# HGRN2 weights inside a chunk: from units of four levels to doubling levels on two column groups of the array

## The chip, the cores and the metric

The kernel runs on one core of a Trainium2 chip. The metric is the device time in microseconds. TensorE is PE, VectorE is DVE, ScalarE is ACT, GpSimd is POOL; PSUM is the memory that PE writes, SBUF the one all engines read.

## The reference

Two layers over 256 tokens of width 2048. Each projects the normalised input, mixes it in two branches of eight heads (a gated delta rule, DN, and HGRN2, HG), projects back, and adds a gated embedding. All is float32. The part that changes is the HGRN2 recurrence within a chunk:

```python
G = jnp.cumsum(log_f, axis=3)
...
rel = masked_exp(causal, G_c[:, :, :, None, :] - G_c[:, :, None, :, :])
A = jnp.einsum("bhrd,bhsd,bhrsd->bhrs", q_c, k_c, rel)
o = (jnp.einsum("bhrd,bhde->bhre", qd_c, state)
     + jnp.einsum("bhrs,bhse->bhre", A, v_c))
```

For every pair r >= s of tokens, A[r, s] is the sum over 128 channels of q[r] k[s] exp(G[r] - G[s]). The exponential depends on r, s and the channel, so A is no plain matrix product. It is one for any block of pairs that have a common token m with s <= m < r: q[r] exp(G[r] - G[m]) times k[s] exp(G[m] - G[s]), and neither exponent is positive.

## The kernel before

Weights of the projections (stages `in`, `out`, `gate`, `up`) are streamed by SP's DMA queue as `raw` tiles. ACT rounds each to F32R (`whi`, L366), DVE forms the rest (`wlo`, L368), and PE sums three products per tile: whi by the activations' high part, wlo by the high part, whi by the low part. Twelve such matmuls, of 512 columns mostly, make a step of `run_step`; `ahead` loads four steps and prepares (whi, wlo) two steps before PE needs them.

The stage `in` runs in 17 chunks of columns. When a chunk is complete, generators (`DN`, `HG`, one per group of two heads and layer, four of each per layer) are started on it. They run between the steps: each `yield` gives a number of steps to wait (`tick`), from the tables `DELAY` and `DELAY_AT`, where "h0a" is step `a` of HG group 0. PE executes in the order written (`keep_in_program_order`); the queues of DVE, ACT and POOL are put in order by a scheduler.

`HG.f_side` makes k and G (a scan along tokens) for a group: two heads by two chunks of 128 tokens, four 128x128 blocks, channels on partitions. `HG.q_side` makes the weights A (tokens s on partitions, r along the free axis), four 128x128 blocks:

- The diagonal: four matmuls of k by q (`pad`), of which the mask `ident` keeps s = r.
- Units u = 1, 4, 16 (`quads`, `quad_products`): in each block of 4u tokens, the pairs of different units of u. K is k decayed to its unit's end (POOL's difference, an Exp, a product with k); Q is q decayed back to the end of each of the three earlier units (three differences, an Exp of 768, three products on DVE). Four matmuls of 192 moving columns, in two PSUM tiles; then DVE places what belongs with `copy_predicated` under masks `ms`, six a unit.
- Level 64 (`halves(64)`): four matmuls with 64 stationary and 64 moving columns; and between the two chunks (`halves(128)`) two of 128 columns (`pax`). POOL makes one of the differences of each.
- `po` multiplies A by the values; `head_norm` follows.

In the profile a matmul's names stand as out <- moving, stationary. Plain F32 matmuls are two records each on PE.

Of the kernel before, what the change touches and what calls it, by code (L numbers as in the profile page):

```python
# [25 lines left out]
def chunk_cols(chunk):  # L26
# [8 lines left out]
    "h": {'c': 1, 'f': 1, 'a': 3, 'u': 1, 'u1': 2, 'u4': 2, 'u16': 2, 'x': 2, 'o': 1, 'y': 2, 'yp': 1, 'q': 0, 'K': 0},  # L35
# [96 lines left out]
UNITS = (1, 4, 16)  # L132


NMASK = 128 + 3 * 192


def const_arrays():
    i = np.arange(128)
    c = np.zeros((128, 4 * 128 + 256), np.float32)  # L140
# [4 lines left out]
    c[:, 512:768] = (np.arange(256) % 128 != 0)[None, :]  # L145
    s, r = i[:, None], i[None, :]
    m = np.zeros((128, NMASK), np.int32)
    m[:, 0:128] = (s // 32 == r // 32) & (s % 32 < 16) & (r % 32 >= 16)
    for n, u in enumerate(UNITS):
        o = 128 + 192 * n  # L150
        for d in (1, 2, 3):
            full = (s // (4 * u) == r // (4 * u)) & (s // u % 4 + d == r // u % 4)
            w = (4 - d) * 128 // 4
            m[:, o:o + w] = full.reshape(128, -1, 4 * u)[:, :, d * u:].reshape(128, w)
            o += w
    return c, m
# [3 lines left out]
def trunk(ctx: ExitStack, tc: tile.TileContext, head, xT, x, pT, W, par, fw, cst, msk, eye, out):  # L160
# [4 lines left out]
    ap_ = pool("acts", 15)  # L165
# [14 lines left out]
    cs = cp.tile([128, 768], F32, name="cs")  # L180
# [68 lines left out]
    keep = cs[:, 512:768]  # L249
# [26 lines left out]
    def bc1(ap, n):  # L276
        return ap.unsqueeze(1).to_broadcast([ap.shape[0], n, ap.shape[1]])
# [549 lines left out]
    class HG:  # L827
# [42 lines left out]
        def q_side(self, qr):  # L870
            l, g, n = self.l, self.g, self.n
            q = mix("hq", 512, 1, n + "q")
            sigmoid(q, qr)
            V.tensor_tensor(q, qr, q, ALU.mult)
            yield self.after("f")
            k, Gc = self.k, self.G
            G4, k4, q4 = v4(Gc), v4(k), v4(q)

            def quads(u):


                nb = 512 // (4 * u)
                vu = lambda ap: ap.rearrange("p (n a b) -> p n a b", a=4, b=u)
                ends = vu(Gc)[:, :, :, u - 1:u]
                K = k
                if u > 1:
                    K = mix("hX", 512, 2, n + f"K{u}")
                    v2 = lambda ap: ap.rearrange("p (n b) -> p n b", b=u)
                    G.tensor_tensor(v2(K), v2(Gc)[:, :, u - 1:u].to_broadcast([128, 512 // u, u]), v2(Gc), ALU.subtract)
                    S.activation(K, K, AF.Exp)  # L890
                    V.tensor_tensor(K, K, k, ALU.mult)
                Q = mix("hQ", 768, 1, n + f"Q{u}")
                Q6 = Q.rearrange("p (n x) -> p n x", x=6 * u)
                o = 0
                for d in (1, 2, 3):
                    w = 4 - d
                    V.tensor_tensor(Q6[:, :, o:o + w * u].rearrange("p n (a b) -> p n a b", b=u), vu(Gc)[:, :, d:],
                                    ends[:, :, :w].to_broadcast([128, nb, w, u]), ALU.subtract)
                    o += w * u
                S.activation(Q, Q, AF.Exp)  # L900
                o = 0
                for d in (1, 2, 3):
                    w = 4 - d
                    V.tensor_tensor(Q6[:, :, o:o + w * u], Q6[:, :, o:o + w * u],
                                    q.rearrange("p (n x) -> p n x", x=4 * u)[:, :, d * u:], ALU.mult)
                    o += w * u
                return K, Q

            def quad_products(u, K, Q):
                for hh in range(2):  # L910
                    pa = pm.tile([128, 512], F32, tag="m", name=n + f"pa{u}_{hh}")
                    for t in range(2):
                        PE.matmul(pa[:, 192 * t:192 * t + 192], v4(K)[:, 2 * hh + t],
                                  Q[:, 384 * hh + 192 * t:384 * hh + 192 * t + 192], start=True, stop=True)
                    P6 = pa[:, :384].rearrange("p (i n x) -> p i n x", i=2, x=6 * u)
                    Av = A[:, 2 * hh:2 * hh + 2].rearrange("p i (n x) -> p i n x", x=4 * u)
                    o, mo = 0, 128 + 192 * UNITS.index(u)
                    for d in (1, 2, 3):
                        w = (4 - d) * u
                        mk = ms[:, mo:mo + 32 * (4 - d)].rearrange("p (n x) -> p n x", x=w)  # L920
                        V.copy_predicated(Av[:, :, :, d * u:], mk.unsqueeze(1).to_broadcast([128, 2, 32 // u, w]),
                                          P6[:, :, :, o:o + w])
                        o += w
                        mo += 32 * (4 - d)

            def halves(hb):

                X = mix("hX", 512, 2, n + f"X{hb}")
                X4 = v4(X)
                if hb == 64:  # L930
                    mid = G4[:, :, 63:64].to_broadcast([128, 4, 64])
                    lo, hi = (slice(None), slice(None), slice(0, 64)), (slice(None), slice(None), slice(64, 128))
                    G.tensor_tensor(X4[lo], mid, G4[lo], ALU.subtract)
                    V.tensor_tensor(X4[hi], G4[hi], mid, ALU.subtract)
                else:
                    lo, hi = (slice(None), slice(0, None, 2)), (slice(None), slice(1, None, 2))
                    G.tensor_tensor(X4[lo], G4[:, 0::2, 127:128].to_broadcast([128, 2, 128]), G4[lo], ALU.subtract)
                    V.tensor_copy(X4[hi], G4[hi])
                S.activation(X, X, AF.Exp)
                V.tensor_tensor(X4[lo], X4[lo], k4[lo], ALU.mult)  # L940
                V.tensor_tensor(X4[hi], X4[hi], q4[hi], ALU.mult)
                return X

            if self.wait("q"):
                yield self.wait("q")
            KQ = quads(1)
            yield self.wait("a")
            A = v4(mix("hA", 512, 1, n + "A"))
            pa = pm.tile([128, 512], F32, tag="m", name=n + "pad")
            for i in range(4):  # L950
                PE.matmul(pa[:, 128 * i:128 * i + 128], k4[:, i], q4[:, i], start=True, stop=True)
            V.tensor_tensor(A, v4(pa), bc1(ident, 4), ALU.mult)
            yield self.wait("u")
            for u in UNITS:
                if self.wait("K"):
                    yield self.wait("K")
                nxt = quads(4 * u) if u < 16 else halves(64)
                quad_products(u, *KQ)
                KQ = nxt
                yield self.wait(f"u{u}")  # L960
            X4 = v4(KQ)
            X = halves(128)
            pa = pm.tile([128, 512], F32, tag="m", name=n + "pa64")
            for i in range(4):
                PE.matmul(pa[0:64, 64 * i:64 * i + 64], X4[:, i, 0:64], X4[:, i, 64:128], start=True, stop=True)
            V.tensor_copy(A[0:64, :, 64:128], pa[0:64, :256].rearrange("p (a b) -> p a b", b=64))
            yield self.wait("x")

            X4 = v4(X)
            pa = pm.tile([128, 512], F32, tag="m", name=n + "pax")  # L970
            for hh in range(2):
                PE.matmul(pa[:, 128 * hh:128 * hh + 128], X4[:, 2 * hh], X4[:, 2 * hh + 1], start=True, stop=True)
            Ax = v4(mix("hAx", 256, 1, n + "Ax"))
            S.copy(Ax, v4(pa)[:, 0:2])
# [293 lines left out]
```

## Time and profile before

| what | before |
|---|---|
| runs | 1299.11 us median of 3 (1297.9 to 1301.97) |
| profiled execution | 1301.33 us, span 1299.6 us |
| PE busy | 98% of the span, 6600 records |
| DVE, ACT, POOL busy | 74%, 60%, 8% |
| granted clock of TensorE, mean | 0.996 |
| longest wait of PE behind the start | 2.9 us, for a wlo of DVE |

In the rows quoted below, a timeline row reads: start in us, duration in us, engine, line, operation, out <- in, partitions x elements, and xN where N records in a row are merged (the duration is then from the first start to the last end); in brackets the idle time of the engine before it and what ended it. A matmul's record is longer than the distance to the next, since matmuls are pipelined. A row of a windows view reads: the stretch, its length, then for each engine its busy time and, in parentheses, its records; then the granted clock of PE and DMA figures. A row of groups reads: busy us, mean ns of one | idle time before them and what ended it.

### The profile page before, as it was taken

How to read it: one execution, taken by the hardware profiler on the slowest of the kernel's cores; microseconds unless marked ns; L12 is line 12 of the kernel's file. 1: busy time of each engine (PE TensorE's matmuls, PEld its weight loads, DVE VectorE, ACT ScalarE, POOL GpSimd, SP SyncE). 2: the span in 40 equal slices, each digit the busy share in tenths (PEclk: the TensorE clock that was granted, in tenths of full speed). 3: DMA queues.
4: the chain of work that ended last, by engine and by line, in shares of the span. 5: the costliest groups of instructions: out<-in, count | busy, mean ns of one | idle time of the engine just before them, and what ended most of it. 6: DMA issues, size and time to landing. Idle time of an engine off the chain costs nothing.

```text
span 1299.6 us, 18426 instructions
## 1 busy us (share of the span) xinstructions
PE 1274.4 (98%) x6600; PEld 1067.9 (82%) x6600; DVE 961.0 (74%) x1800; ACT 779.4 (60%) x1392; POOL 103.0 (8%) x86
## 2 busy tenths in 40 slices
PE   8999999999999999999999999999999999999996
PEld 7987788888888888888888887888888888888885
DVE  7788877976798766546668897788877968565475
ACT  7665765666665654447557666657566666444464
POOL 0101010010001110000001100111100002000010
PEclk9999999999999999999999999999999999999998
DMA  8565455445455455565555454544455444655563
GB/s 281 180 208 169 153 158 162 133 151 182 154 163 162 132 163 178 187 192 184 188 184 174 155 162 159 170 142 141 156 184 176 145 163 133 198 179 181 192 194 130
DMA packets 78748, 221.02 MB, mean 170 GB/s; under 512 B 15552, under 2 KB 25152, under 8 KB 78656
## 3 DMA queue, kind: packets, MB, share of 16 engines
q1 hardware_dynamic: 59840, 212.36, 50.4%
q10 hardware_dynamic: 18816, 7.48, 2.2%
q8 instruction: 52, 0.85, 0.3%
q14 instruction: 40, 0.33, 0.1%
HBM read 215.09 MB, written 4.72 MB: 169 GB/s over the span
## 4 chain that ended last, share of the span: by engine, by line
PE 78%; DVE 14%; ACT 3%; issue 2%; DMA 2%; SPq 0%; ACTq 0%; DVEq 0%
PE gate L309 13%; PE out L309 12%; PE in1dv L309 6%; PE in1hf L309 5%; PE in0dk L309 5%; PE in0dv L309 5%; PE in0hf L309 5%; PE in1dk L309 5%; DVE wlo L368 4%; PE in1hi L309 4%; PE in0hi L309 3%; PE up L309 2%; PE in0dz L309 1%; PE in1dz L309 1%; ACT whi L366 1%
## 5 line engine op out<-in xcount | busy, mean ns | idle before, releaser
L368 DVE TENSOR_TENSOR wlo<-raw,whi 128x1024 fp32r<-128x1024 f32 (+1 forms) x394 | 481.8, 1226 | 237.2 <-ACT whi L366 236.2
L366 ACT ACTIVATE whi<-raw 128x1024 fp32r<-128x1024 f32 (+1 forms) x394 | 413.3, 1051 | 342.7 <-PE out L309 83.2
L309 PE MATMUL in1hf<-whi,n1hi 128*128 128x512 f32 x128 | 52.0, 407 | 0.0
L309 PE MATMUL in1hi<-whi,n1hi 128*128 128x512 f32 x128 | 52.0, 406 | 0.0
L309 PE MATMUL in1dk<-whi,n1hi 128*128 128x512 f32 x128 | 51.1, 399 | 0.0
L309 PE MATMUL in1dk<-wlo,n1hi 128*128 128x512 f32 x128 | 50.1, 392 | 0.9 <-DVE wlo L368 0.8
L309 PE MATMUL in1hi<-wlo,n1hi 128*128 128x512 f32 x128 | 50.1, 391 | 0.6 <-DVE wlo L368 0.6
L309 PE MATMUL gate<-whi,g0hi 128*128 128x512 f32 x128 | 50.1, 392 | 0.0
L309 PE MATMUL in1hf<-whi,n1lo 128*128 128x512 f32 x128 | 50.1, 391 | 0.0
L309 PE MATMUL in1hi<-whi,n1lo 128*128 128x512 f32 x128 | 50.0, 391 | 0.0
L309 PE MATMUL in1hf<-wlo,n1hi 128*128 128x512 f32 x128 | 49.9, 390 | 0.0
L309 PE MATMUL in1dk<-whi,n1lo 128*128 128x512 f32 x128 | 49.9, 390 | 0.0
L309 PE MATMUL gate<-whi,g1hi 128*128 128x512 f32 x128 | 49.9, 390 | 0.0
L309 PE MATMUL gate<-whi,g0lo 128*128 128x512 f32 x128 | 49.8, 389 | 0.0
L309 PE MATMUL gate<-wlo,g0hi 128*128 128x512 f32 x128 | 49.8, 389 | 0.0
L309 PE MATMUL gate<-whi,g1lo 128*128 128x512 f32 x128 | 49.8, 389 | 0.0
L309 PE MATMUL gate<-wlo,g1hi 128*128 128x512 f32 x128 | 49.8, 389 | 0.0
L309 PE MATMUL in1dv<-whi,n1hi 128*128 128x512 f32 (+1 forms) x128 | 48.7, 380 | 0.0
L309 PE MATMUL in1dv<-wlo,n1hi 128*128 128x512 f32 (+1 forms) x128 | 46.6, 364 | 0.1
L309 PE MATMUL in1dv<-whi,n1lo 128*128 128x512 f32 (+1 forms) x128 | 46.5, 364 | 0.0
L309 PE MATMUL in0dk<-wlo,n0hi 128*128 128x512 f32 x96 | 38.2, 398 | 2.9 <-DVE wlo L368 2.9
L309 PE MATMUL in0hf<-whi,n0hi 128*128 128x512 f32 x96 | 39.0, 406 | 0.0
(1620 smaller groups left out, 3353.8 us busy)
## 6 DMA issues: line engine op xcount, KB each, us to landing
raw<-W SPq DMA_DIRECT2D x384, 512.0 KB, 3.5
raw<-W SPq DMA_DIRECT2D x7, 544.0 KB, 3.7
h<-x SPq DMA_DIRECT2D x4, 512.0 KB, 5.6
xt<-xT SPq DMA_DIRECT2D x3, 512.0 KB, 7.3
out_dram<-h SPq DMA_DIRECT2D x6, 256.0 KB, 2.2
fw<-fw ACTq DMA_DIRECT2D x2, 512.0 KB, 4.9
pin<-pT ACTq DMA_DIRECT2D x2, 256.0 KB, 3.0
out_dram<-h ACTq DMA_DIRECT2D x2, 256.0 KB, 2.9
```

The source lines that it names most:

```text
L309: return tc.keep_in_program_order(nc.tensor.matmul(*a, **k))
L366: S.activation(hi[:, sl], raw[:, sl], AF.Copy)
L368: V.tensor_tensor(lo[:, sl], raw[:, sl], hi[:, sl].bitcast(F32), ALU.subtract)
```

## The change

The weights of a chunk are made in doubling levels u = 1, 2, 4, 8, 16, 32, 64 (and 128 between the chunks). At level u, each block of 2u tokens has a lower half, whose k is decayed to that half's end, and an upper half, whose q is decayed back to it; `factors` writes both into one tile X in place of K and Q. For u below 64 a 128-token block is two matmuls, one for each 64 tokens, with 64 stationary columns (all of X's tokens there) and as moving columns the 32 of the upper halves. Their outputs lie on PSUM partitions 0 to 63 and 64 to 127, so they use the array's columns 0 to 63 and 64 to 127. The diagonal is in the first of them: q and the level-1 factors stand side by side in a tile of 96 columns per 64 tokens. The masks become six of 32 columns, and results gather in `Ad` (two 64x64 blocks one above the other), which ACT copies to `hA`, a tile that is allocated once and zeroed below its diagonal. Levels are done in the pairs (1, 2), (4, 8), (16, 32), (64, 128), four bursts on PE. All differences are on DVE.

`DELAY` and `DELAY_AT` are set anew, for DN's steps too, and the pool of activations has 13 buffers for 15. The diff, cut:

```diff
-    "h": {'c': 1, 'f': 1, 'a': 3, 'u': 1, 'u1': 2, 'u4': 2, 'u16': 2, 'x': 2, 'o': 1, 'y': 2, 'yp': 1, 'q': 0, 'K': 0},
+    "h": {'c': 1, 'f': 1, 'a': 4, 'u1': 3, 'u4': 3, 'u16': 3, 'o': 2, 'y': 2, 'yp': 1, 'q': 0},
...
-UNITS = (1, 4, 16)
-NMASK = 128 + 3 * 192
+UNITS = (1, 2, 4, 8, 16, 32)
+NMASK = 128 + 32 * len(UNITS)
...
-    ap_ = pool("acts", 15)
+    ap_ = pool("acts", 13)
...
+    hA = cp.tile([128, 4, 128], F32, name="hA")
     def clear_scratch():
+        G.memset(hA[64:128, :, 0:64], 0.0)
...
+            q8 = mix("hq", 768, 1, n + "q").rearrange("p (a c) -> p a c", c=96)
+            q = q8[:, :, 0:64]
...
+            def factors(us):
+                X = mix("hX", 1024, 2, n + f"X{us[0]}")[:, :512 * len(us)]
+                xs = [X[:, 512 * j:512 * j + 512] for j in range(len(us))]
+                for u, x in zip(us, xs):
+                    ends = lo(Gc, u)[:, :, u - 1:u].to_broadcast([128, 256 // u, u])
+                    V.tensor_tensor(lo(x, u), ends, lo(Gc, u), ALU.subtract)
+                    if u < 128:
+                        V.tensor_tensor(hi(x, u), hi(Gc, u), ends, ALU.subtract)
+                    else:
+                        V.tensor_copy(hi(x, u), hi(Gc, u))
+                S.activation(X, X, AF.Exp)
+                for u, x in zip(us, xs):
+                    V.tensor_tensor(lo(x, u), lo(x, u), lo(k, u), ALU.mult)
...
+                    V.tensor_tensor(hx, hx, hx_q, ALU.mult)
+                return [v4(x) for x in xs]
+            def products(us, xs, pa, o=0):
+                for j, (u, x) in enumerate(zip(us, xs)):
+                    for i in range(4):
+                        for b in (0, 64):
+                            xb = x[:, i, b:b + 64]
+                            c = o + 128 * j + 32 * i
+                            PE.matmul(pa[b:b + 64, c:c + 32], xb,
+                                      xb.rearrange("p (n a b) -> p n a b", a=2, b=u)[:, :, 1], start=True, stop=True)
+            def place(us, ws):
...
+                    V.copy_predicated(Ad.rearrange("p i (n a b) -> p i n a b", a=2, b=u)[:, :, :, 1],
+                                      mk.unsqueeze(1).to_broadcast([128, 4, 32 // u, u]),
+                                      w.rearrange("p i (n b) -> p i n b", b=u))
...
+            x1 = q8[:, :, 64:96]
+            V.tensor_tensor(x1, c32(hi(Gc, 1)), c32(lo(Gc, 1)), ALU.subtract)
+            S.activation(x1, x1, AF.Exp)
+            V.tensor_tensor(x1, x1, hq(1)[:, :, :, 0], ALU.mult)
+            xs = factors((2,))
             yield self.wait("a")
+            Ad = mix("hAd", 256, 1, n + "Ad").rearrange("p (i c) -> p i c", i=4)
+            pa = bank("1")
             for i in range(4):
+                for b in (0, 64):
+                    PE.matmul(pa[b:b + 64, 96 * i:96 * i + 96], k4[:, i, b:b + 64], q8[:, 2 * i + b // 64, :],
+                              start=True, stop=True)
+            nxt = factors((4, 8))
+            products((2,), xs, pa, 384)
+            w1 = pa[:, :384].rearrange("p (i c) -> p i c", c=96)
+            V.tensor_tensor(Ad, w1[:, :, 0:64], bc1(ident64, 4), ALU.mult)
+            place((1, 2), (w1[:, :, 64:96], v32(pa[:, 384:512])))
+            yield self.wait("u1")
+            for us, then in (((4, 8), (16, 32)), ((16, 32), (64, 128))):
+                xs, nxt = nxt, factors(then)
+                pa = bank(f"{us[0]}")
+                products(us, xs, pa)
+                place(us, (v32(pa[:, 0:128]), v32(pa[:, 128:256])))
+                yield self.wait(f"u{us[0]}")
...
+            A = hA
+            for b in (0, 64):
+                S.copy(A[b:b + 64, :, b:b + 64], Ad[b:b + 64])
+            S.copy(A[0:64, :, 64:128], pa[0:64, :256].rearrange("p (a b) -> p a b", b=64))
```

How instructions move, for the first group of the first layer (`hg00`). On PE before, the diagonal's four matmuls stand ahead of a step; a burst of the units stands further on (first lines the diagonal, then the first unit):

```order
L309 MATMUL in0dk_1_1030<-wlo_1114,n0hi_294 128x512
L309 MATMUL in0dk_1_1030<-whi_1113,n0lo_295 128x512
L309 MATMUL hg00pad<-hg00q,hg00k 128x128 x4
L309 MATMUL in0dk_0_1029<-whi_1132,n0hi_300 128x512
L309 MATMUL in0dk_0_1029<-wlo_1133,n0hi_300 128x512
...
L309 MATMUL in0dk_1_1030<-whi_1186,n0lo_386 128x512
L309 MATMUL hg00pa_0_1252<-hg00Q_1085,hg00k 128x192 x2
L309 MATMUL hg00pa_1_1258<-hg00Q_1085,hg00k 128x192 x2
L309 MATMUL in0dv_0_1267<-whi_1204,n0ahi_126 128x512
```

and after, the first burst (diagonal with level 1, then level 2) and the second (levels 4 and 8):

```order
L309 MATMUL in0dk_1_1032<-wlo_1137,n0hi_301 128x512
L309 MATMUL in0dk_1_1032<-whi_1136,n0lo_302 128x512
L309 MATMUL hg00pa_1200<-hg00q,hg00k 64x96 x8
L309 MATMUL hg00pa_1200<-hg00X_1091 64x32 x8
L309 MATMUL in0dk_0_1031<-whi_1165,n0hi_380 128x512
L309 MATMUL in0dk_0_1031<-wlo_1166,n0hi_380 128x512
...
L309 MATMUL in0dv_1_1270<-whi_1232,n0alo_128 128x512
L309 MATMUL hg00pa_1301<-hg00X_1209 64x32 x16
L312 MATMUL dn01pkc<-cs,dn01kqet 128x128 x4
```

The first burst now stands one step later than the diagonal did, and already holds two levels. (The step's weights are wlo_1133 before and wlo_1137 after.)

On DVE before, from the scan that ends G (shown as SCALAR_TENSOR_TENSOR at L866) to the next weights:

```order
L874 TENSOR_TENSOR hg00q<-hg00pq,hg00q 128x512
L866 SCALAR_TENSOR_TENSOR hg00G<-cs,hg00fsg 128x256 x2
L897 TENSOR_TENSOR hg00Q_1085<-hg00G 128x128x3
L897 TENSOR_TENSOR hg00Q_1085<-hg00G 128x128x2
L897 TENSOR_TENSOR hg00Q_1085<-hg00G 128x128
L368 TENSOR_TENSOR wlo_1133<-raw_1093,whi_1132 128x1024
L904 TENSOR_TENSOR hg00Q_1085<-hg00Q_1085,hg00q 128x128x3
```

and after:

```order
L866 SCALAR_TENSOR_TENSOR hg00G<-cs,hg00fsg 128x256 x2
L368 TENSOR_TENSOR wlo_1137<-raw_1097,whi_1136 128x1024
L940 TENSOR_TENSOR hg00q<-hg00G 128x8x32
L899 TENSOR_TENSOR hg00X_1091<-hg00G 128x128x2
L901 TENSOR_TENSOR hg00X_1091<-hg00G 128x128x2
L597 TENSOR_SCALAR neG<-eG 128x2
L942 TENSOR_TENSOR hg00q<-hg00q 128x8x32
L368 TENSOR_TENSOR wlo_1166<-raw_1115,whi_1165 128x1024
L906 TENSOR_TENSOR hg00X_1091<-hg00X_1091,hg00k 128x128x2
L913 TENSOR_TENSOR hg00X_1091<-hg00X_1091,hg00q 128x128x2
L899 TENSOR_TENSOR hg00X_1209<-hg00G 128x64x4
```

The weights wlo of that step stand ahead of the differences, no longer behind them.

Further on, in group 2 of the first layer (`hg02`), on DVE after, a long run between two weights:

```order
L368 TENSOR_TENSOR wlo_4064<-raw_3978,whi_4063 128x1024
L955 TENSOR_TENSOR hg02Ad<-hg02pa_4031,cs 128x256
L906 TENSOR_TENSOR hg02X_4040<-hg02X_4040,hg02k 128x64x4
L913 TENSOR_TENSOR hg02X_4040<-hg02X_4040,hg02q 128x64x4
L906 TENSOR_TENSOR hg02X_4040<-hg02X_4040,hg02k 128x32x8
L913 TENSOR_TENSOR hg02X_4040<-hg02X_4040,hg02q 128x32x8
L930 COPY_PREDICATED hg02Ad<-ms,hg02pa_4031 128x128
L899 TENSOR_TENSOR hg02X_4138<-hg02G 128x16x16
L930 COPY_PREDICATED hg02Ad<-ms,hg02pa_4031 128x64x2
L901 TENSOR_TENSOR hg02X_4138<-hg02G 128x16x16
L899 TENSOR_TENSOR hg02X_4138<-hg02G 128x8x32
L901 TENSOR_TENSOR hg02X_4138<-hg02G 128x8x32
```

Between this wlo and the next stand the diagonal's product, levels 4 and 8's products, two placings, and the differences of levels 16 and 32. POOL has 57 rows after for 88 before.

More of the change, by code (lines that the diff above doesn't have):

```diff
@@ L145, in const_arrays @@
     c[:, 512:768] = (np.arange(256) % 128 != 0)[None, :]
+    c[:, 768:832] = i[:, None] % 64 == np.arange(64)[None, :]
     s, r = i[:, None], i[None, :]
@@ L149, in const_arrays @@
     for n, u in enumerate(UNITS):
[L150 to L155, printed above, removed]
+        low = (s % 64 // (2 * u) == np.arange(32)[None, :] // u) & (s % (2 * u) < u)
+        m[:, 128 + 32 * n:160 + 32 * n] = low
     return c, m
@@ L179, in trunk @@
     pr = cp.tile([128, NPAR], F32, name="pr")
-    cs = cp.tile([128, 768], F32, name="cs")
+    cs = cp.tile([128, 832], F32, name="cs")
     ms = cp.tile([128, NMASK], I32, name="ms")
@@ L248, in trunk @@
     ident, ones, SL, UI = (cs[:, 128 * j:128 * j + 128] for j in range(4))
-    keep = cs[:, 512:768]
+    keep, ident64 = cs[:, 512:768], cs[:, 768:832]
     epsc = cp.tile([128, 1], F32, name="epsc")
@@ L876, in q_side @@
             k, Gc = self.k, self.G
[L877 to L942, printed above, removed]
+            k4 = v4(k)
@@ new lines, in q_side, with hq @@
+            lo = lambda ap, u: ap.rearrange("p (n a b) -> p n a b", a=2, b=u)[:, :, 0]
+            hi = lambda ap, u: ap.rearrange("p (n a b) -> p n a b", a=2, b=u)[:, :, 1]
+            def hq(u):
+                if u < 64:
+                    return q.rearrange("p a (n c b) -> p a n c b", c=2, b=u)[:, :, :, 1]
+                return q.rearrange("p (n c a) b -> p n c a b", c=2, a=u // 64)[:, :, 1]
+            def factors(us):
[8 more added lines that the diff above has]
+                        V.tensor_copy(hi(x, u), hi(Gc, u))
+                S.activation(X, X, AF.Exp)
+                for u, x in zip(us, xs):
+                    V.tensor_tensor(lo(x, u), lo(x, u), lo(k, u), ALU.mult)
+                    hx = hi(x, u)
+                    if u < 64:
+                        hx = hx.rearrange("p (a n) b -> p a n b", a=8)
+                    elif u == 128:
+                        hx = hx.rearrange("p n (a b) -> p n a b", b=64)
+                    hx_q = hq(u) if u != 64 else hq(u)[:, :, 0]
+                    V.tensor_tensor(hx, hx, hx_q, ALU.mult)
+                return [v4(x) for x in xs]
@@ L954, in q_side @@
[L954 to L963, printed above, removed]
-            for i in range(4):
-                PE.matmul(pa[0:64, 64 * i:64 * i + 64], X4[:, i, 0:64], X4[:, i, 64:128], start=True, stop=True)
@@ new lines, in q_side @@
+            xs = nxt
+            pa = bank("64")
+            for i in range(4):
+                PE.matmul(pa[0:64, 64 * i:64 * i + 64], xs[0][:, i, 0:64], xs[0][:, i, 64:128], start=True, stop=True)
+            for hh in range(2):
+                PE.matmul(pa[:, 256 + 128 * hh:384 + 128 * hh], xs[1][:, 2 * hh], xs[1][:, 2 * hh + 1],
+                          start=True, stop=True)
+            A = hA
+            for b in (0, 64):
+                S.copy(A[b:b + 64, :, b:b + 64], Ad[b:b + 64])
```

28 lines of the change are left out of this document (12 added, 16 removed), and 16 rows, old and new, of the table DELAY_AT.

## The prediction

> **What bounds the kernel now.** I read the page's busy table first, then the list of waits on PE, then the timeline of PE around the bursts that the change replaces, and last the vector engine where PE waited.
>
> ```profile
> span 1299.6 us, 18426 instructions
> PE 1274.4 (98%) x6600; PEld 1067.9 (82%) x6600; DVE 961.0 (74%) x1800; ACT 779.4 (60%) x1392; POOL 103.0 (8%) x86
> ...
> PE in0dk L309 <- DVE wlo L368: 2.9, 1, 2.9
> PE in0hi L309 <- DVE wlo L368: 0.9, 1, 0.9
> PE in1dk L309 <- DVE wlo L368: 0.8, 1, 0.8
> PE in1hi L309 <- DVE wlo L368: 0.6, 1, 0.6
> ```
>
> PE is busy for 98% of the span, so a microsecond taken out of PE's own stream is a microsecond of the whole. DVE at 74% and ACT at 60% cost something only where PE waits for them; the four wlo rows are such places, 5.2 us together. The profiled run took 1301.33 us beside a span of 1299.6, and stands 2.2 us above the median of the three runs, 1299.11; I work out a difference on the profiled one and apply it to the median.
>
> **What the replaced matmuls cost.** A matmul of plain F32 is two records on PE (x8 below is four matmuls). I price a burst by the start of the weight matmul after next behind it, less the start of the last one ahead, less two ordinary slots. The first two rows are one slot apart: 0.23 us.
>
> ```profile
> 154.63 0.39 PE L309 MATMUL in0hi<-wlo,n0hi 128*128 128x512 f32 x1
> 154.86 0.39 PE L309 MATMUL in0hi<-whi,n0lo 128*128 128x512 f32 x1
> 155.18 0.68 PE L309 MATMUL hg00pa<-hg00X 128*64 128x64 f32 x8
> 155.79 0.50 PE L309 MATMUL in0hi<-whi,n0hi 128*128 128x512 f32 x1
> 156.12 0.39 PE L309 MATMUL in0hi<-wlo,n0hi 128*128 128x512 f32 x1
> ...
> 112.62 0.39 PE L309 MATMUL in0dk<-whi,n0lo 128*128 128x512 f32 x1
> 112.85 1.46 PE L309 MATMUL hg00pa<-hg00Q,hg00k 128*128 128x192 f32 x8
> 114.01 0.53 PE L309 MATMUL in0dv<-whi,n0ahi 128*128 128x512 f32 x1
> 114.38 0.39 PE L309 MATMUL in0dv<-wlo,n0ahi 128*128 128x512 f32 x1
> ...
> 161.97 0.39 PE L309 MATMUL in0hi<-whi,n0lo 128*128 128x512 f32 x1
> 162.19 0.61 PE L309 MATMUL hg00pax<-hg00X 128*128 128x128 f32 x4
> 162.55 0.48 PE L309 MATMUL in0hi<-whi,n0hi 128*128 128x512 f32 x1
> 162.87 0.39 PE L309 MATMUL in0hi<-wlo,n0hi 128*128 128x512 f32 x1
> ...
> 40.64 0.40 PE L309 MATMUL in0dk<-whi,n0lo 128*128 128x512 f32 x1
> 40.87 0.95 PE L309 MATMUL x2s<-onec,x 128*128 128x1 f32 x8
> 41.69 0.47 PE L309 MATMUL in0dk<-whi,n0hi 128*128 128x512 f32 x1
> 42.00 0.39 PE L309 MATMUL in0dk<-wlo,n0hi 128*128 128x512 f32 x1
> ```
>
> A unit's burst of 192 columns takes 114.38 - 112.62 - 0.46 = 1.30 us, 0.163 a pass. The two cross-chunk matmuls take 162.87 - 161.97 - 0.46 = 0.44, 0.11 a pass. With one moving column instead of 128 a pass still takes (42.00 - 40.64 - 0.46) / 8 = 0.113: below 128 columns the pass costs the loading of its 128 stationary columns, whatever moves. So a pass with 64 stationary columns has a floor of half that, 0.056. The level-64 burst, 156.12 - 154.86 - 0.46 = 0.80, is then 8 x 0.056 and 0.35 for going from the whole array to 64 columns and back.
>
> One HGRN2 group now pays 3 x 1.30 for the units, twice 0.44 for the diagonal (four matmuls of 128 columns, two bursts' worth of the 0.44), 0.80 and 0.44: 6.02 us. There are eight groups.
>
> **The change on PE.** It makes 54 small matmuls out of 22, 40 of them with 32 moving columns and 8 with 96, all on half the array's columns, the halves in turn. What it is worth hangs on whether the halves run at the same time. The nearest row is the solve's 32x32 burst, four matmuls on one block of the array, then four on another:
>
> ```profile
> 139.54 0.39 PE L309 MATMUL in0dv<-whi,n0lo 128*128 128x512 f32 x1
> 139.86 0.59 PE L309 MATMUL dn00pp<-dn00T,dn00Bt 32*32 32x32 f32 x16
> 140.37 0.50 PE L309 MATMUL in0dv<-whi,n0hi 128*128 128x512 f32 x1
> 140.71 0.40 PE L309 MATMUL in0dv<-wlo,n0hi 128*128 128x512 f32 x1
> ...
> 139.85:140.00 0.15, 0.14 (x4) 1.00 0.75 294
> 139.85:140.13 0.28, 0.27 (x12) 1.00 0.58 223
> 139.85:140.30 0.45, 0.44 (x16) 1.00 0.60 230
> ```
>
> The last three rows count that burst's passes on PE in growing windows: 4 start in the first 0.15 us, 8 in the next 0.13, 4 in the last 0.17. The middle is where the second block has begun and the first is not done: two blocks go through at double the rate, their loads included. Those blocks share neither rows nor columns; the new ones share all 128 rows. That leaves two ends: full overlap, or none.
>
> With full overlap a pair takes one slot. First burst: 8 pair slots of 96 columns at half of 0.163, 0.081, and 8 of 32 columns at the floor 0.056, with 0.35 for the switch: 1.45 us. Levels 4 and 8 together, and 16 and 32 together: 16 x 0.056 + 0.35 = 1.25 each. Level 64 and the cross-chunk pair stay, 0.80 + 0.44. Sum 5.19 instead of 6.02: 0.83 x 8 = 6.6 us off. With no overlap the 48 pairs pay double, 0.65 + 5 x 0.45 = 2.90 more a group: 8.09, 16.6 us onto the whole. I take full overlap, because the only row with two blocks in flight shows it. The strided moving columns of level 2 and up are unpriced; streaming 32 columns is a sixth of 0.163, 0.027, so it could double unseen under the 0.056.
>
> The rule that speaks against it is in the Trainium skill, page TensorE: Matmul & The Clock Gate, section Part 3, The mechanism: a weight load overlaps running matmuls only when the two use different row groups. The new halves share every row, so by that rule they go in turn and the sum is the 16.6 us loss. The trace does not bear it out for one block: passes of 192 follow each other at 0.163 us without their loads showing. For two column halves no run here shows it; the page TensorEngine Tiling (Array Packing), Key Properties, says that different tiles load and multiply in parallel.
>
> **The other engines.** Three kinds of vector work go: the nine strided differences, the eighteen predicated copies, and POOL's four differences, which move to DVE.
>
> ```profile
> L921 DVE COPY_PREDICATED hg00A<-ms,hg00pa 128x192 f32<-128x192 int32 (+2 forms) x18 | 5.4, 355 | 1.2 <-PE hg00pa L309 1.2
> L897 DVE TENSOR_TENSOR hg00Q<-hg00G 128x384 f32<-128x384 f32 (+2 forms) x9 | 5.2, 627 | 0.0
> L940 DVE TENSOR_TENSOR hg00X<-hg00X,hg00k 128x256 f32<-128x256 f32 x2 | 0.8, 422 | 0.5 <-ACT hg00X L939 0.5
> ```
>
> Six predicated copies of 128 elements replace eighteen, at most 6 x 0.36 = 2.1 for 5.4. Seven levels of four 256-element operations cost 28 x 0.42 = 11.8, with two more for level 1, in place of the Q and K work. DVE gets lighter by a few us a group. Exps of 1024 replace those of 768; three small copies come to ACT, which has 40% free. All that runs beside PE and counts nothing, except where PE was waiting:
>
> ```profile
> 99.06 2.90 DVE L897 TENSOR_TENSOR hg00Q<-hg00G 128x384 f32<-128x384 f32 x3
> 101.87 1.21 DVE L368 TENSOR_TENSOR wlo<-raw,whi 128x1024 fp32r<-128x1024 f32 x1
> ...
> 103.14 0.50 PE L309 MATMUL in0dk<-wlo,n0hi 128*128 128x512 f32 x1 [2.90 <-DVE wlo L368]
> ...
> 104.65:108.03 3.38, 3.38 (x9) 2.62 (x8) 3.38 (x5) 2.70 (x4) 0.00 (x0) 0.50 0.72 230
> ```
>
> The 2.90 us of differences stand ahead of the wlo that PE needs, and PE idles as long. The window row behind it then has a granted clock of 0.50 for 3.38 us, another 1.69 lost: 4.6 in all. In the new order that wlo stands ahead of the first difference, so this wait goes. What is late next is the first burst itself: behind that wlo DVE has three differences, a product, the next wlo and two products, 6 x 0.42 + 1.21 = 3.7 us, and the exps between; PE has one step of twelve matmuls, 12 x 0.23 = 2.7, to cover it. I keep 1.5 us of waiting and no clock loss: 3.1 off. The other three wlo waits (0.9, 0.8, 0.6) fall in groups 2 and 0 of the two layers, behind the same three differences; half of their 2.3 goes, 1.1. New waits: between two wlo at the start of level 16 DVE now has a mask product, four products, two predicated copies and four differences, 9 x 0.42 + 2 x 0.36 + 1.21 = 5.7 us against two steps of PE, 5.5, which is how far wlo is prepared ahead. I bound what that opens by 0 and 5 us in all and take 1.0, near the low end because DVE as a whole has less to do.
>
> The retuned delays shift bursts by a tick or two; order and count of the weight matmuls stay. Two fewer buffers of activations put one ACT split of each layer's residual behind ten matmuls of the output stage, 10 x 0.23 = 2.3 us; wlo is 5.5 ahead, so I cost it at nothing, and at 4 us in all if that cover is gone. Mask loads shrink and ride with SP's early loads, at nothing.
>
> Sum: -6.6 - 3.1 - 1.1 + 1.0 = -9.8, so 1289.3 us.
>
> **The rivals.** *The halves go in turn* (slower): PE's stream grows by 16.6, less the 3.2 from the waits: 1312.5. For it: nothing here shows blocks on the same rows overlapping. Against: the middle window row. It decides from the point where more than (0.83 + 0.40) / 2.90 = 42% of the overlap is lost, 0.40 being a group's share of the 3.2. Chance 0.14. *Half the overlap*: 1.45 - 0.83 = 0.62 a group, +5.0 - 3.2, about 1301; spread 1296 to 1306; 0.10. *The bursts shrink but waits return*: new waits of 4 to 5 instead of 1 and the small ones stay: about 1294.5, from 1292 to 1297; for it speaks the 5.7 against 5.5; 0.16. *All waits go*: -6.6 - 4.6 - 2.3, 1285.6; 0.12. The forecast, 1286.5 to 1292: 0.48.
>
> **How the numbers follow.** A change of under 0.3%, 3.9 us, can't be told from none here. Faster holds the forecast, "all waits go" and two thirds of "waits return": 0.71. The same: the rest of that and half of "half the overlap", 0.10. Slower: 0.19. The range 1283.5 to 1301 leaves out the serial case and half of the half overlap, with a little below.
>
> **What would show it.** PE records go from 6600 to 7112 (256 matmuls more, two records each). Right: sixteen 32-column matmuls, x32, take about 1.25 us by the same subtraction, the first burst 1.45; wrong at 2.15 and 2.55. The 2.90 wait and the clock of 0.50 near 104 us are gone, and PE's wlo waits sum to under 3 us. A serial pair slot, or a wlo late in every group, would make the prediction wrong.

## The result, and the profile after

| | before | after |
|---|---|---|
| median of 4 runs | 1299.73 us (1297.9 to 1301.97) | 1285.93 us (1285.03 to 1286.61) |
| profiled execution, span | 1301.33 us, 1299.6 | 1285.03 us, 1283.3 |

The ratio is 0.9887, interval 0.9872 to 0.9901: 13.8 us faster. The prediction said 1289.3, within 1283.5 to 1301; the direction is as forecast, and the time is that of the rival "all waits go", 1285.6. (The two profiled executions lie 16.3 us apart, as before's was one of its longer runs and after's its shortest; sizes below go by the medians.)

The head of the page and the complete list of waits on PE, both of the changed kernel. A row of waits reads: who waited and at which line <- what ended the wait: us in total, number of waits, longest in us.

```profile
span 1283.3 us, 19310 instructions
PE 1262.2 (98%) x7112; PEld 1054.2 (82%) x7112; DVE 925.7 (72%) x1728; ACT 785.2 (61%) x1400; POOL 61.5 (5%) x55
```

```profile
PE in0dz L309 <- ACT whi L238: 6.7, 3, 4.5
PE dn02pv L312 <- DVE dn02vac L770: 0.7, 1, 0.7
PE dn11pp L309 <- DVE dn11T L726: 0.7, 1, 0.7
PE dn01pp L309 <- DVE dn01T L726: 0.7, 1, 0.7
PE in1dk L309 <- DVE wlo L368: 0.2, 1, 0.2
```

PE has the 7112 records that were expected. Its four wlo waits, 5.2 us before, are one of 0.2. The kernel before also had six rows that the prediction did not show, behind its four, two of 0.6, two of 0.4 and two of 0.2; one of each, from its list of waits:

```profile
PE dn11pvc L312 <- ACT dn10Tt L743: 0.6, 1, 0.6
...
PE dn11pp L309 <- DVE dn11T L726: 0.4, 1, 0.4
...
PE dn02pv L312 <- DVE dn02vac L770: 0.2, 1, 0.2
```

The six sum to 2.4; the three DN rows after sum to 2.1. So behind the start PE's listed waits go from 7.6 to 2.3 us. (The start's wait, in0dz, is before the changed code and differs from run to run: 5.9 in a second run of this same kernel.)

The new bursts, in PE's timeline: the first (diagonal with levels 1 and 2) and the third (16 and 32).

```profile
101.81 0.39 PE L309 MATMUL in0dk<-whi,n0lo 128*128 128x512 f32 x1
102.13 0.88 PE L309 MATMUL hg00pa<-hg00q,hg00k 128*64 128x96 f32 x16
102.84 0.61 PE L309 MATMUL hg00pa<-hg00X 128*64 128x32 f32 x16
103.37 0.50 PE L309 MATMUL in0dk<-whi,n0hi 128*128 128x512 f32 x1
103.71 0.39 PE L309 MATMUL in0dk<-wlo,n0hi 128*128 128x512 f32 x1
...
122.64 0.39 PE L309 MATMUL in0dv<-whi,n0lo 128*128 128x512 f32 x1
122.96 1.12 PE L309 MATMUL hg00pa<-hg00X 128*64 128x32 f32 x32
124.01 0.50 PE L309 MATMUL in0dv<-whi,n0hi 128*128 128x512 f32 x1
124.35 0.39 PE L309 MATMUL in0dv<-wlo,n0hi 128*128 128x512 f32 x1
```

By the prediction's subtraction they take 103.71 - 101.81 - 0.46 = 1.44 us and 124.35 - 122.64 - 0.46 = 1.25. The second (4 and 8), at 111.76, has DN's matmuls right behind it; from its first pass to them it takes 1.05 us, as the third does to the weight matmul behind it (122.96 to 124.01). The last one (64 and 128), where weight matmuls stand on both sides of it (group 2, at 411 us), takes 1.25 as well. With the 1.25 three times a group pays 5.19 (5.21 unrounded), against 6.02.

The place of the old 2.90 us stall, on DVE after, and the window in which the clock had been 0.50:

```profile
98.05 1.19 DVE L368 TENSOR_TENSOR wlo<-raw,whi 128x1024 fp32r<-128x1024 f32 x1
...
99.51 0.41 DVE L899 TENSOR_TENSOR hg00X<-hg00G 128x256 f32<-128x256 f32 x1
...
102.05 0.41 DVE L913 TENSOR_TENSOR hg00X<-hg00X,hg00q 128x256 f32<-128x256 f32 x1
```

```profile
104.65:108.03 3.38, 3.38 (x16) 2.81 (x15) 3.38 (x9) 2.37 (x3) 0.00 (x0) 1.00 0.69 194
```

The wlo is done at 99.24, and the last product for the first burst at 102.46; PE comes to the matmuls that need it at 102.84. Nobody waits, by 0.4 us. The clock is 1.00, and 16 matmuls run in the window where 9 did.

So the rows show: bursts, (6.02 - 5.21) x 8 = 6.5; listed waits 7.6 - 2.3 = 5.3; the clock near 104 us, 1.7. Together 13.5, near the 13.8 of the medians, but in part by luck: they are read from the pair that lies 16.3 us apart, and the wait at the start is 1.1 longer after (5.6 before). PE's busy time fell by 12.2 us (1274.4 to 1262.2), and the bursts and the clock are 8.2 of them. Where the other 4.0 lie was not traced. One part may be that bursts which stand next to each other share the way from the whole array and back: in group 2 the third burst follows a 32x32 burst of the solve, and both together take 402.36 - 400.13 - 0.46 = 1.77 us, where alone they take 0.71 (the solve's burst in the prediction, 140.71 - 139.54 - 0.46) and 1.25.

### The profile page after: what moved, and what is told of

The parts are those of the page before. It is cut to its first block, busy times and chain, and to the rows that moved or that the text cites. A ratio compares the mean times of both kernels' runs of the same rounds, so it can differ in the third digit from the quotient of the medians.

```text
span 1283.3 us, 19310 instructions
## 1 busy us (share of the span) xinstructions
PE 1262.2 (98%) x7112; PEld 1054.2 (82%) x7112; DVE 925.7 (72%) x1728; ACT 785.2 (61%) x1400; POOL 61.5 (5%) x55
## 4 chain that ended last, share of the span: by engine, by line
PE 91%; DVE 5%; ACT 1%; issue 1%; DMA 0%; SPq 0%; DVEq 0%; ACTq 0%
PE out L309 14%; PE gate L309 14%; PE in1hf L309 6%; PE in0hf L309 6%; PE in0dv L309 6%; PE in1dv L309 6%; PE in0dk L309 6%; PE in1dk L309 6%; PE in0hi L309 6%; PE in1hi L309 5%; PE up L309 2%; DVE wlo L368 1%; PE in0dz L309 1%; PE in1dz L309 1%; ACT whi L366 1%
## 5 line engine op out<-in xcount | busy, mean ns | idle before, releaser
L309 PE MATMUL in0hi<-whi,n0hi 128*128 128x512 f32 x96 | 38.5, 401 | 0.0
```

The source lines that it names most:

```text
L309: return tc.keep_in_program_order(nc.tensor.matmul(*a, **k))
```

## The experiments

The theory: both column halves run at the same time, loads included, if their matmuls alternate; the waits went because DVE no longer stands in front of the weights. Rivals: the small passes are cheap by themselves, without overlap; and the waits went for another reason (the retuned delays, POOL). Medians in us; each is also compared with the kernel before on the same chip.

| run | time | ratio to before |
|---|---|---|
| halves in runs | 1300.13 (one run) | - |
| lower differences on POOL | 1292.56 | 0.9928 (0.9913 to 0.9943) |
| first burst one step earlier | 1300.15 | 0.9993 (0.9982 to 1.0004) |
| before, all differences on DVE | 1295.45 | 0.9949 (0.9932 to 0.9966) |
| levels 4 to 32 in one burst | 1281.39 | 0.9847 (0.9829 to 0.9864) |
| diagonal apart | 1287.03 | 0.9891 (0.9872 to 0.9910) |
| changed kernel again | 1284.26 | 0.9874 (0.9856 to 0.9892) |
| two bursts | 1290.27 | 0.9923 (0.9909 to 0.9936) |
| two bursts, later DN step | 1284.43 | 0.9879 (0.9862 to 0.9896) |

**Halves in runs.** The same matmuls, all of columns 0 to 63 first, then all of 64 to 127; for levels 64 and 128 nothing changes.

```diff
-                for j, (u, x) in enumerate(zip(us, xs)):
-                    for i in range(4):
-                        for b in (0, 64):
+                for b in (0, 64):
+                    for j, (u, x) in enumerate(zip(us, xs)):
+                        for i in range(4):
...
-            for i in range(4):
-                for b in (0, 64):
+            for b in (0, 64):
+                for i in range(4):
```

> The changed kernel with the same matmuls in another order: within each burst all matmuls of one column half first, then all of the other, instead of in turn. Theory 'the two halves run at the same time': only around the one changeover some passes overlap (about 4 in the solve's 32x32 burst), so a burst of 32 passes takes about 28 x 0.056 + 0.35 = 1.9 us instead of 1.25, the first burst about 2.0 instead of 1.45; in all some 8 x (2 x 0.65 + 0.5) = 14 us more, about 1300. Rival 'a pass of half width with 32 columns is simply cheap, about 0.028 us, with no overlap': the order doesn't matter, bursts stay at 1.25 and 1.45 and the time at 1286.

PE's timeline at the same third burst:

```profile
124.80 0.39 PE L309 MATMUL in0dv<-whi,n0lo 128*128 128x512 f32 x1
125.12 1.84 PE L309 MATMUL hg00pa<-hg00X 128*64 128x32 f32 x32
126.89 0.50 PE L309 MATMUL in0dv<-whi,n0hi 128*128 128x512 f32 x1
127.23 0.39 PE L309 MATMUL in0dv<-wlo,n0hi 128*128 128x512 f32 x1
```

127.23 - 124.80 - 0.46 = 1.97 instead of 1.25, with the same 32 passes; the first burst 1.83 instead of 1.44. A group has two of the one and one of the other: (2 x 0.72 + 0.39) x 8 = 14.6 us, and the span, 1298.4, is 15.1 longer than the changed kernel's. The overlap is shown by the rows of the bursts, and that it comes from taking the halves in turn; the time is of a single run and only agrees with it. Without it the whole change comes out at 1300.13, where the kernel before had 1301.51 on that chip.

**Lower differences on POOL**, as the kernel before had them:

```diff
-                    V.tensor_tensor(lo(x, u), ends, lo(Gc, u), ALU.subtract)
+                    G.tensor_tensor(lo(x, u), ends, lo(Gc, u), ALU.subtract)
```

> The changed kernel with the differences of the lower halves (seven of 256 elements a group) on POOL again. Theory 'POOL working on the same data slowed DVE and made wlo late before': DVE's differences beside POOL take about 1 us instead of 0.42, PE's waits for wlo come back by 2 to 5 us, time 1288 to 1291. Rival 'it was the place of wlo behind three differences in DVE's order alone': DVE has less to do, waits stay near 0, time 1286 or below.

It costs 6.6 us by the medians, but not where I looked. The waits on PE behind the start, of the first layer (the second has the same two):

```profile
PE dn01pp L309 <- DVE dn01T L726: 1.6, 1, 1.6
...
PE in0dv L309 <- ACT dn01kqet L544: 1.5, 1, 1.5
```

Two wlo waits of 0.2 follow. DVE has less to do than in the changed kernel (921.4 us busy against 925.7), and yet PE's waits are 6.6 in place of 2.3, for DN's work; the other 2.3 us of the cost stand in no row of waits. Of these 1.7 are the clock: behind the wait for dn01T, which ends at 213.38, it is near half for 3.4 us.

```profile
213.99:217.40 3.41, 3.41 (x38) 3.15 (x36) 2.56 (x6) 1.57 (x3) 0.95 (x2) 0.51 0.64 217
```

What DVE keeps gets slower beside POOL; the groups of the upper differences of one HG group, first here, then in the changed kernel (columns: shortest, median, longest, in ns):

```profile
L901 DVE TENSOR_TENSOR hg00X<-hg00G x6: 405/432/867, 99.4 to 115.4; 128x256 f32<-128x256 f32 x6
```

```profile
L901 DVE TENSOR_TENSOR hg00X<-hg00G x6: 399/405/417, 99.8 to 120.1; 128x256 f32<-128x256 f32 x6
```

The two waits come by different ways. Ahead of dn01T, three operations of DVE that start while POOL works (207.16 to 210.32) take 0.84, 1.63 and 0.83 us, where the changed kernel's take 0.42, 1.22 and 0.42; that is 1.2 us, less the 0.34 of the difference that left DVE, and the wait is 0.9 longer. For dn01kqet the way leads over ACT: its Exp of hg00X waits 3.3 us for POOL's differences, to 104.93, the next Exp starts at 110.24, and dn01kqet behind it at 111.20. In the changed kernel ACT makes dn01kqet from 107.79 on, ahead of that Exp. So this run prices POOL's place in the queues as well as what it does to DVE.

**First burst one step earlier**, the delay that the kernel before had:

```diff
-    "h": {'c': 1, 'f': 1, 'a': 4, 'u1': 3, 'u4': 3, 'u16': 3, 'o': 2, 'y': 2, 'yp': 1, 'q': 0},
+    "h": {'c': 1, 'f': 1, 'a': 3, 'u1': 3, 'u4': 3, 'u16': 3, 'o': 2, 'y': 2, 'yp': 1, 'q': 0},
...
-    "h0a": 5, "h0yp": 2,
+    "h0a": 4, "h0yp": 2,
...
-    "h2a": 5, "h2o": 1, "h2yp": 2,
+    "h2a": 4, "h2o": 1, "h2yp": 2,
```

> The changed kernel with the delay of step a one step shorter in all groups (4 and 5 become 3 and 4). Theory 'the new delays are what keeps PE from waiting at the first burst': its products on DVE are done just as PE gets there, so one step (2.7 us) earlier PE waits some 2 us in the groups where DVE is full (0 and 2 of both layers), 1289 to 1294. Rival 'DVE being lighter is what took the waits away, the delays have slack': no new waits, 1286.

The whole gain is lost, more than I expected. Some of the longest waits on PE:

```profile
PE hg12pa L309 <- DVE hg12q L942: 1.5, 1, 1.5
PE hg00pa L309 <- DVE hg00q L942: 1.4, 1, 1.4
PE hg10pa L309 <- DVE hg10q L942: 1.3, 1, 1.3
PE hg00pa L309 <- DVE hg00X L913: 0.9, 1, 0.9
```

With the smaller rows they sum to some 12 us behind the start, where the changed kernel has 2.3; the mean granted clock is 0.994 against 0.997, 0.003 x 1298 = 3.9. Of that 3.4 lie behind the two waits of hg00:

```profile
101.50:108.30 6.80, 6.42 (x29) 5.24 (x30) 4.74 (x12) 1.06 (x1) 0.00 (x0) 0.50 0.60 198
```

The burst catches the factors unready in most groups. The retuned delay is thus a necessary part of the change: without it new waits use up what the shorter bursts gain.

**Before, with all differences on DVE.** Only this of the change, put on the kernel before (its bursts, delays and order stay):

```diff
-                    G.tensor_tensor(v2(K), v2(Gc)[:, :, u - 1:u].to_broadcast([128, 512 // u, u]), v2(Gc), ALU.subtract)
+                    V.tensor_tensor(v2(K), v2(Gc)[:, :, u - 1:u].to_broadcast([128, 512 // u, u]), v2(Gc), ALU.subtract)
...
-                    G.tensor_tensor(X4[lo], mid, G4[lo], ALU.subtract)
+                    V.tensor_tensor(X4[lo], mid, G4[lo], ALU.subtract)
...
-                    G.tensor_tensor(X4[lo], G4[:, 0::2, 127:128].to_broadcast([128, 2, 128]), G4[lo], ALU.subtract)
+                    V.tensor_tensor(X4[lo], G4[:, 0::2, 127:128].to_broadcast([128, 2, 128]), G4[lo], ALU.subtract)
```

> The kernel before with its four POOL differences a group on DVE, all else as before. Theory 'the 2.90 us of three differences ahead of wlo were slow because POOL worked beside them': they take 0.57 + 0.42 + 0.28 = 1.3 us, PE's wait of 2.9 falls to about 1.3, the clock of 0.50 behind it does not come, and the waits of 0.9, 0.8 and 0.6 vanish: 4 to 6 us faster, 1294 to 1296. Rival 'the order, not POOL': the three still take over 2.5 us, or the added DVE work makes wlo as late: 1299 or slower.

6.1 us faster, with more instructions on DVE (1832 for 1800). DVE's timeline at the stall, and the window behind it:

```profile
99.88 1.23 DVE L897 TENSOR_TENSOR hg00Q<-hg00G 128x384 f32<-128x384 f32 x3
101.01 1.22 DVE L368 TENSOR_TENSOR wlo<-raw,whi 128x1024 fp32r<-128x1024 f32 x1
```

```profile
103.00:108.50 5.50, 5.38 (x24) 4.08 (x23) 5.50 (x10) 3.40 (x5) 0.00 (x0) 1.00 0.65 201
```

The three differences that took 2.90 us take 1.23. In the kernel before, POOL ran beside them; its timeline there:

```profile
99.11 2.60 POOL L889 TENSOR_TENSOR hg00K<-hg00G 128x512 f32<-128x512 f32 x2 [23.08 <-DVE hg00G L866]
```

The 2.90 wait becomes 1.3, the clock stays at 1.00, and the wlo waits of 0.8 and 0.6 in layer 1 fall to 0.2 or vanish; the 0.9 stays. In all PE's listed waits behind the start go from 7.6 to 4.8 us, so of the 9.3 us that the kernel before lost in waits and clock (7.6 and 1.7), 4.5 were POOL's doing by these rows; the time moved by 6.1. That DVE's differences are slow beside POOL's, which I had in the diff and in the rows, is the rule of the Trainium skill, page SBUF — State Buffer, section Who interferes with whom: a vector instruction with two SBUF inputs contends with a GpSimd instruction that reads SBUF. The trace agrees, 1.23 against 2.90.

**Levels 4 to 32 in one burst.** The second and third burst become one; the factors of 16 and 32 are made a stage earlier.

```diff
-            for us, then in (((4, 8), (16, 32)), ((16, 32), (64, 128))):
-                xs, nxt = nxt, factors(then)
-                pa = bank(f"{us[0]}")
-                products(us, xs, pa)
-                place(us, (v32(pa[:, 0:128]), v32(pa[:, 128:256])))
-                yield self.wait(f"u{us[0]}")
+            xs = nxt + factors((16, 32))
+            yield self.wait("u4")
+            us = (4, 8, 16, 32)
+            pa = bank("4")
+            products(us, xs, pa)
+            nxt = factors((64, 128))
+            place(us, [v32(pa[:, 128 * j:128 * j + 128]) for j in range(4)])
+            yield self.wait("u16")
```

> The changed kernel with levels 4, 8, 16 and 32 in one burst (one PSUM bank, 64 matmuls in turn) instead of two bursts of 32 passes each. Theory 'each trip from the whole array to half columns and back costs 0.35 us by itself': one trip less a group, the burst takes 32 x 0.056 + 0.35 = 2.15 us instead of 2 x 1.25, 8 x 0.35 = 2.8 us less in all, about 0.22% under the changed kernel. Rival 'the 0.35 is the filling of the first passes and is paid per level, or the chain to A gets longer and PE waits for it': no gain, or some us slower.

```profile
121.61 0.39 PE L309 MATMUL in0dv<-whi,n0lo 128*128 128x512 f32 x1
121.93 2.06 PE L309 MATMUL hg00pa<-hg00X 128*64 128x32 f32 x64
123.91 0.50 PE L309 MATMUL in0dv<-whi,n0hi 128*128 128x512 f32 x1
124.25 0.39 PE L309 MATMUL in0dv<-wlo,n0hi 128*128 128x512 f32 x1
```

124.25 - 121.61 - 0.46 = 2.18 for what took 2 x 1.25: a trip from the whole array to its halves and back costs 0.32 us, as the prediction had it (0.35). Eight trips saved are 2.6 us, and the median is 2.9 below the changed kernel on the same chip. The intervals of the two ratios overlap, so it is the rows that show the gain, and the time agrees. 1281.39 us is the lowest median of the study.

**Diagonal apart.** The 96 moving columns are split into 64 and 32, eight matmuls more a group:

```diff
-                    PE.matmul(pa[b:b + 64, 96 * i:96 * i + 96], k4[:, i, b:b + 64], q8[:, 2 * i + b // 64, :],
+                    PE.matmul(pa[b:b + 64, 64 * i:64 * i + 64], k4[:, i, b:b + 64], q8[:, 2 * i + b // 64, 0:64],
...
+            for i in range(4):
+                for b in (0, 64):
+                    PE.matmul(pa[b:b + 64, 256 + 32 * i:288 + 32 * i], k4[:, i, b:b + 64],
+                              q8[:, 2 * i + b // 64, 64:96], start=True, stop=True)
```

> The changed kernel with the diagonal's 64 columns and level 1's 32 columns as matmuls of their own instead of one of 96. Theory 'below the load of 64 stationary columns a pass costs 0.058, whatever moves, above it the moving columns': 8 pair slots at 0.081 become 16 at 0.058, the first burst 1.45 + 0.28 = 1.73 us, 2.2 us more in all than the changed kernel. Rival 'what counts is moving columns': the sum of columns is the same, the burst stays at 1.45 and the time with it.

The first burst takes, by the same subtraction in its timeline (104.10 - 101.93 - 0.46), 1.71 us instead of 1.44, which is 2.2 us over the eight groups; the medians differ by 2.8, with intervals that overlap. The burst has 48 passes, 16 of them with 64 moving columns, at (1.71 - 0.32) / 48 = 0.029. A pass of 32 costs (1.25 - 0.32) / 32 = 0.029 in turn as well, so 16 of them by themselves are 0.47 us; riding on the diagonal's loads, the same columns cost 0.47 - 0.27 = 0.20.

**The changed kernel again**, beside these on the same chip, unedited:

> The changed kernel as it is, on the same chip as the two runs beside it, so that differences of 2 to 3 us can be told. All theories: a ratio to the kernel before of 0.987 to 0.990, and bursts of 1.45 and 1.25.

1284.26 us and a ratio of 0.9874, in the interval of the first measurement; behind the start its waits are the four of the first measurement, 0.7 three times and 0.2.

**Two bursts.** Levels 1 to 8 in one, 16 to 128 in the other (and the step `o` of group 2 at its default):

```diff
             yield self.wait("a")
+            nxt = factors((4, 8))
+            yield self.wait("u16")
...
-            nxt = factors((4, 8))
             products((2,), xs, pa, 384)
+            products((4, 8), nxt, pb)
...
+            place((4, 8), (v32(pb[:, 0:128]), v32(pb[:, 128:256])))
+            x16 = factors((16, 32))
             yield self.wait("u1")
-            for us, then in (((4, 8), (16, 32)), ((16, 32), (64, 128))):
...
+            xs = factors((64, 128))
+            yield self.wait("u4")
+            pb, pa = bank("16"), bank("64")
+            products((16, 32), x16, pb)
             for i in range(4):
                 PE.matmul(pa[0:64, 64 * i:64 * i + 64], xs[0][:, i, 0:64], xs[0][:, i, 64:128], start=True, stop=True)
```

> The changed kernel with two bursts a group instead of four: levels 1, 2, 4 and 8 (and the diagonal) in the first, levels 16, 32, 64 and the cross-chunk pair in the second; the waits between them add up to the same number of steps. Theory 'a trip to half columns and back costs 0.35 us and nothing else in PE's stream changes': two trips less a group, 8 x 0.70 = 5.6 us less than the changed kernel, ratio to the kernel before about 0.983 (the changed one stood at 0.987). Rival 'the factors of four levels come late and PE waits at the longer bursts': PE waits for hg tiles show up and the ratio is 0.985 or above.

```profile
221.01 0.39 PE L309 MATMUL in0dk<-whi,n0lo 128*128 128x512 f32 x1
221.33 0.88 PE L309 MATMUL hg01pa<-hg01q,hg01k 128*64 128x96 f32 x16
222.04 1.54 PE L309 MATMUL hg01pa<-hg01X 128*64 128x32 f32 x48
223.51 0.50 PE L309 MATMUL in0dv<-whi,n0ahi 128*128 128x512 f32 x1
223.85 0.39 PE L309 MATMUL in0dv<-wlo,n0ahi 128*128 128x512 f32 x1
```

The bursts do what they should, 223.85 - 221.01 - 0.46 = 2.38, and the other 2.19, 4.57 a group instead of 5.21. But the kernel is 6.0 us slower than the changed one, and neither theory had the place: PE waits for DN's tiles, not for hg tiles. On DVE the operations of hg01X stand between DN's, and dn02kq starts at 240.52, behind two of them and five operations of dn02qac; in the changed kernel it starts at 237.55, behind two of dn02qac. From its waits, and from its windows (granted clock 0.53):

```profile
PE dn02ssk L312 <- DVE dn02kq L619: 2.6, 1, 2.6
PE dn12ssk L312 <- DVE dn12kq L619: 2.6, 1, 2.6
PE in1dv L309 <- DVE wlo L368: 0.9, 1, 0.9
PE in0dv L309 <- DVE wlo L368: 0.9, 1, 0.9
```

```profile
242.00:245.50 3.50, 3.50 (x11) 2.68 (x10) 2.75 (x8) 3.11 (x13) 0.00 (x0) 0.53 0.26 73
```

Each of the two waits of 2.6 is followed by some 3.4 us at half the clock, 1.7 more: 2 x 4.3 + 1.8 for wlo is 10.4 lost for 8 x 0.64 = 5.1 gained, a net of 5.3 of the 6.0.

**Two bursts, later DN step.** One step more before that DN work (`"d2k"` 3 to 4), the two bursts kept:

> The two-burst kernel with the delay of step k of DN group 2 one step longer (3 becomes 4), which puts dn02ssk behind twelve more weight matmuls. Theory 'the two-burst kernel lost its gain in one place per layer, the 2.6 us wait for dn02kq and the halved clock behind it': both go, some 8 us off its 0.9923, ratio 0.983 to 0.986. Rival 'DVE is full there, the wait moves to the next matmul that needs it': the ratio stays above 0.990 and another row of DVE stands in PE's waits.

```profile
PE dn02pg L309 <- DVE dn02kq L619: 1.0, 1, 1.0
PE dn12pg L309 <- DVE dn12kq L619: 1.0, 1, 1.0
PE in1dv L309 <- DVE wlo L368: 0.9, 1, 0.9
```

5.8 of the 6.0 us come back, and the halved clock is gone (1.00 from 238 to 249 us), which bears out the cause. The time is still only that of the changed kernel: of the 5.1 us of shorter bursts, 3.8 are waited for here (2 x 1.0 and 2 x 0.9). The ratio fell between what the two theories said; one delay does not make DVE's order that of the changed kernel again.

## Why the prediction came out as it did

- *The bursts.* 1.45, 1.25, 1.25 and 1.24 predicted, 1.44, 1.25, 1.25 and 1.25 measured; 6.6 us predicted, 6.5 measured. The step that carried it, full overlap of two blocks that share all rows, rested on one row of two blocks that share none; it was a bet that paid off, and the run with the halves in runs shows it. The strided moving columns, unpriced, cost nothing seen: levels 4 and 8 and levels 16 and 32 take the same 1.05 from their first pass to the matmul behind them. The rule that I weighed against it (the Trainium skill, TensorE: Matmul & The Clock Gate, Part 3, The mechanism: loads overlap only on other row groups) does not hold here: 1.25 in turn against 1.97 in runs.
- *The waits, the mis-sized term.* "I keep 1.5 us of waiting", "half of their 2.3 goes", "take 1.0": -3.2 net. The runs showed -7.0: all of the first 4.6 (2.90 and the clock), 2.1 of the 2.3, and 0.3 in DN's rows (2.4 to 2.1) where I had put 1.0 of new waits. The 1.5 that I kept stood on 3.7 us of DVE work against 2.7 of PE's. In the run the DVE work took 102.46 - 99.24 = 3.2, since its operations start 0.34 us apart and not 0.42; and PE needs the last of it only for the second part of the burst, at 102.84, after the first sixteen records that need q alone.
- *What I read wrongly in the row.* I took the 2.90 us as what three differences cost, and POOL's four differences as work that DVE gets on top. They were slow because POOL ran beside them; on DVE alone they take 1.23. In the kernel before, taking POOL out is worth 6.1 us, interval 4.4 to 8.8 (0.9949, 0.9932 to 0.9966). From there to the change are another 0.9949 - 0.9887 = 0.0062, 8.1 us, by two measurements on different chips, each uncertain by some 2 us: room for the bursts' 6.5 and a little of waits. The wait of 2.90 went as forecast, but the new order, to which I gave all of it, is not shown to be what took it: with the old order and the differences on DVE it is 1.3, and the clock stays at 1.00.
- *What came to ACT, the fewer activation buffers, the masks*: no row of waits on PE names them. POOL's busy time fell from 103.0 to 61.5 us.
- *The rival that happened.* "All waits go" had 0.12, since I asked what wait comes next at each place but not whether the wait's cause, rather than its place in the order, was removed.
- *What stays open.* How the 5.3 us of listed waits divide between the new order, the delays and POOL: the order was changed only together with the rest, of the delays only the first burst's by itself. The wait of 0.9 that stays with the differences on DVE is gone in the changed kernel, so something else of the change took it. The 4.0 us of PE's busy time that the rows do not place stay open too.

## What to carry to other kernels

Small matmuls on two column halves of the array overlap, loads and all, if they are issued in turn, and each trip between whole array and halves has a price of its own, so bursts are worth joining as far as the vector engine can have their operands ready together without holding up its other work. A vector operation that takes twice its usual time in a trace should be compared with what GpSimd does in the same microseconds before it is taken as a price. When a burst gets shorter or needs its operands earlier, move it by a step first: here one step was worth the whole gain.

## What the runs showed of the hardware

- Two column halves on the same 128 rows run at once: 32 passes of 32 columns in 1.25 us in turn, 1.97 one half after the other, of which 0.32 is the switch. A pass on 64 columns is then (1.97 - 0.32) / 32 = 0.052 us alone, half of the 0.113 of 128 columns, and in turn passes with 64 moving columns take the same 0.029 as passes with 32: the stationary columns set it, not those that move.
- PE waits of 2.90 us (before) and 2.63 (two bursts) were each followed by some 3.4 us at a granted clock near 0.50; waits of 1.3 (differences on DVE) and 1.0 (later DN step) were not. The length of one wait does not decide it: in the first layer of the run with the earlier first burst, waits of 1.38 and 0.92, with 0.88 us of work between them, were followed by 6.8 us at 0.50, and in the first layer of the run with the lower differences on POOL one of 1.61 by 3.4 us at 0.51, while the like waits in the second layers of both left the clock at 1.00. The Trainium skill (TensorE: Matmul & The Clock Gate, Part 1, What's actually happening) puts the step down at an idle window of about 3.4 us; here shorter ones did it.
- Differences on DVE that share their time with POOL's took twice as long and more: 2.90 us for three against 1.23, and at most 867 ns for one against 417.
